# A fused RWKV-7 / short-convolution layer on one core: reordering transfers at the seam of two phases, and moving the preparation of four output weights to GpSimd

## The chip, the core and the metric

The kernel runs on one core of a Trainium2 chip. The core has five engines that each take their instructions in order: TensorE (PE in the profile, with its weight loads listed as PEld), VectorE (DVE), ScalarE (ACT), GpSimd (POOL) and SyncE (SP), which here issues nearly all transfers between the chip's memory (DRAM) and the on-chip memory (SBUF). A transfer queue is in order as well: if its next transfer has to wait, all behind it wait too. The metric is the device time of one execution, in microseconds (us), as a median over runs.

## What is computed

One layer on 128 context tokens and 2048 latent tokens of width 1024. The normalised, modulated input h goes through one input projection. Half of its channels (8 heads of 64) go through RWKV-7 mixing in both directions, the other half through a short gated convolution; both halves are gated, joined, and go through the output projection `w_out`. Cut to what matters here:

```python
def step(S, inp):                       # RWKV-7, per head, S is 64 x 64
    r_t, w_t, k_t, v_t, kk_t, a_t = inp
    s_kk = einsum('bdhij,bdhj->bdhi', S, kk_t)
    S = S * w_t[..., None, :] - s_kk[..., :, None] * (kk_t * a_t)[..., None, :] \
        + v_t[..., :, None] * k_t[..., None, :]
    return S, einsum('bdhij,bdhj->bdhi', S, r_t)
...
ya = ya * silu(g_a)                     # after a group norm and a bonus term
yb = b_gate * short_conv(c_gate * u_conv) * silu(g_b)
u = concatenate([ya, yb], -1) @ w_out
y = rmsnorm(x + gate * u)
```

The latent scans start from cached states `state_wkv`. The outputs are y of both kinds of tokens and the final states of the context.

## The kernel before

The scan is not run token by token. Tokens are cut into chunks of 64. Within a chunk the delta rule needs the inverse of a triangular 64 x 64 matrix per chunk, head and direction; between chunks only the state S is passed on. Matrix products in full precision are made of three products of a high and a low part (`hi`, `lo`), the high part being a copy into the type fp32r and the low part the difference.

**Phase 1** (`phase1`) makes the projections. The tokens stand in six blocks, taken as three pairs; for each pair the dense products of all column blocks are made (L166 to L168, tiles `mm...`), and their results are turned into the operands of the scan (`scr_ops`, `scr_at`, `scr_lo`, `scr_vt` in DRAM) or into the convolution (`convB` makes the products `mmc` and `mmu` and the taps, L523 to L541; `gateB` makes `mmgb`, `mmb` and the gates, L570 to L585). In the last pair the convolution of column groups 1, 2 and 3 stands at the very end: twelve steps, each one call of `convB` or `gateB` for one block. After each of the twelve, one step of the generator `early` of phase 2 is taken. This stretch, about 890 to 1005 us, is the seam.

**Phase 2** (`phase2`) goes through 17 stages, each of 16 chunks (two directions). Stage s needs, in order: its operands (`partL`), the inverses of 32 x 32 triangles (`partI` on GpSimd, which calls `load_I`, `solve_steps` and stores to `scr_zt`), the products F and G and their evacuation (`partW`, L1041 and L1048), the 64 x 64 inverse from the 32 x 32 ones (`partU`), X and E (`partB`), and the chain of states (`partS`, L1147). `main` has one round per stage; the letters of `ROUND` give the order in which the products of stage s and s+1 are mixed, and `mm` ties these products into one order by hand (`O.line`). The copy with a mask (L1072) stands once in every round, which makes it a mark of the rounds.

In the seam, `early` does what can be done ahead: it sets up the tiles (L785), centres the cached states (`center_states`: load L977, reduce L979, subtraction L981, store L982), lets GpSimd invert for stages 2 and 5, lets VectorE invert for stages 3 and 4 (`by_vector`, whose working space is the part of the tiles `fg` that stage 1 will use later for its operands), and does stage 0's `partW` and `partU` and some of `partB`. GpSimd's diagonal tile and the centring's mean share one buffer (tag `dgp`).

Stage 1's operands are loaded by `load_half` (L998), into the part of `fg` in which VectorE has inverted; so they wait for those inverses and for their stores (L955).

**Phase 3** (`phase3`) is the output projection in 17 tiles of 128 tokens. `ahead` prepares the weights of the convolution half during phase 2's last rounds (`load_k`: high part L1360, low part L1361, for k = 4 to 7), splits the mixed values of the first two tiles (`load_m`: L1372, L1373) and makes their products (`psa`, from L1380 on); these products are not in the hand-made order. `tail` does the rest; there the other four weights are already split by GpSimd for the low part (L1361) and ScalarE for the high part.

What sets the order: the program gives priorities by the order in which instructions are written, and a planner orders each engine's queue by simulating the program with its own costs. An instruction whose inputs are ready in that simulation can be put before others that were written earlier. `behind(r, ins)` adds an edge for the planner alone: r is not ordered before ins, though no wait is made for it on the chip. `K.dense` is the last dense product written so far. Waits on the chip follow from the data and from the reuse of buffers.

Of the kernel before, what the change touches and what calls it, by code (L numbers as in the profile page):

```python
# [6 lines left out]
F32 = mybir.dt.float32  # L7
F32R = mybir.dt.float32r
BF16 = mybir.dt.bfloat16
AF = mybir.ActivationFunctionType  # L10
ALU = mybir.AluOpType
# [743 lines left out]
def phase2(K):  # L755
    nc, tc, A, S = K.nc, K.tc, K.A, K.S
    V, G, P, T = nc.vector, nc.gpsimd, nc.scalar, nc.tensor
    D = nc.sync.dma_start
    B = Ctx()
    O = Ctx()  # L760
# [101 lines left out]
    def half(g, n):  # L862

        h = n if g.d == 0 else 1 - n
        return slice(h * 4, h * 4 + 4)
# [66 lines left out]
    def solve_steps(eng, s, ab, zt, tmp, dg, after):  # L932

        zf = zt[:].rearrange("p a b -> p (a b)")
        behind(eng.memset(zt[:], 0.0), after)
        for h in range(2):
            eng.memset(zf[h * 64:(h + 1) * 64, h:512:34], 1.0)

        eng.tensor_copy(dg[:], ab[:].rearrange("p j i -> p (j i)")[:, 1:1024:66])
        eng.tensor_scalar(zf[0:64, 1:512:34], dg[0:64], -1.0, None, ALU.mult)  # L940
        tv = tmp[:].rearrange("p (j m) -> p j m", m=16)
        eng.tensor_tensor(tv, ab[:, :, 0:32:2], dg[:].unsqueeze(1).broadcast_to((128, 32, 16)), ALU.mult)
        eng.tensor_tensor(ab[:, :, 1:32:2], ab[:, :, 1:32:2], tv, ALU.subtract)
        for m in range(15):
            j, kn, n = 2 * m, m + 1, 30 - 2 * m
            tv = tmp[:, :kn * 2 * n].rearrange("p (q r i) -> p q r i", r=2, i=n)
            eng.tensor_tensor(tv, ab[:, j:j + 2, j + 2:32].unsqueeze(1).broadcast_to((128, kn, 2, n)),  # L947
                              zt[:, :kn, j:j + 2].unsqueeze(3).broadcast_to((128, kn, 2, n)), ALU.mult)
            for r in range(2):
                last = eng.tensor_tensor(zt[:, :kn, j + 2:32], zt[:, :kn, j + 2:32], tv[:, :, r], ALU.subtract).ins  # L950
            if m % 4 == 0:
                yield
        if eng is G:
            O.solved = last
        (G.dma_start if eng is G else D)(S["zt"][s].rearrange("h u s b q i -> (h u s b) (q i)"), zf)  # L955

    def by_vector(s, d):

# [15 lines left out]
    def center_states():  # L974

        x = O.rI.tile([64, 16, 64], F32, tag="ab", name="st0", bufs=1)
        D(x[:], A["st0"].rearrange("k d h v -> k (d h) v"))  # L977
        mn = O.rI.tile([64, 16], F32, tag="dgp", name="st0mean", bufs=1)
        V.tensor_reduce(mn[:], x[:], mybir.AxisListType.X, ALU.add)  # L979
        V.tensor_scalar(mn[:], mn[:], -1.0 / 64, None, ALU.mult)  # L980
        V.tensor_tensor(x[:], x[:], mn[:].unsqueeze(2).broadcast_to((64, 16, 64)), ALU.add)  # L981
        D(S["sti"].rearrange("k d h v -> k (d h) v"), x[:])  # L982
# [8 lines left out]
    def load_half(g, us, D):  # L991

        p, c0 = g.units[us.start]
        src = S[f"ops{g.d}"][1:3]
        for h in range(2):
            dst = B.fg[g.d][H[h], :, g.op, h, us].rearrange("c k u t -> c k (u t)")
            if g.blk is not None:
                D(dst, src[:, p * 128 + h * 64:p * 128 + h * 64 + 64, c0 * 64:(c0 + 4) * 64].rearrange("k c t -> c k t"))  # L998
            else:
                for k in range(2):  # L1000
                    D(dst[:, k].rearrange("c (g t) -> c g t", t=128), src[k, :, 0:128].rearrange("(g h c) t -> h c g t", h=2, c=64)[h][:, p:p + 2])
# [9 lines left out]
    def partW(s, st):  # L1011

        D = nc.sync.dma_start if s else P.dma_start
        for g in st.g:
            g.E, g.F = [], []
            g.op = 1 + s % 2
            g.io = slice(0, g.op + 1, g.op)
            g.gs, g.fs = B.fg[g.d][:, 0], B.fg[g.d][:, 1]
        for n in range(2):
            for g in st.g:  # L1020
                load_half(g, half(g, n), D)
            if n == 0:
                if s:
                    states(s, st)
                st.zc = tl([128, 16, 32], "zc", 1, O.r0)
                for h in range(2):
                    D(st.zc[h:128:2], S["zt"][s][h].rearrange("u s b q i -> (s b q) u i"))

            def product(k, x, nm):
                ps = [ps_tile([128, 4, 128], f"ps{nm}{s}_{gi}_{n}") for gi in range(2)]  # L1030
                for i in range(4):
                    for gi, g in enumerate(st.g):
                        u = half(g, n).start + i
                        for h in range(2):
                            mm(ps[gi][place(g.d, h), i, :].rearrange("p (b t) -> p b t", b=2), g.ops[H[h], k, u, :], B.fg[g.d][H[h], x, g.io, h, u])
                return ps

            ps = product(0, 1, "F")
            for gi, g in enumerate(st.g):
                g.F.append(tl([128, 4, 128], "F", 4, O.r0))  # L1040
                V.tensor_tensor(g.F[n][:], ps[gi][:], B.mF[:, g.d].unsqueeze(1).broadcast_to((128, 4, 128)), ALU.mult)  # L1041
            yield
            ps = product(1, 0, "G")
            for gi, g in enumerate(st.g):
                us = half(g, n)
                for h in range(2):
                    r = place(g.d, h)
                    V.tensor_tensor(g.gs[H[1 - h], g.op, h, us], ps[gi][r, :, 64:128], B.mG[r, g.d].unsqueeze(1).broadcast_to((64, 4, 64)), ALU.mult)  # L1048
                    copy(g.gs[H[1 - h], 0, h, us], ps[gi][r, :, 0:64])
            yield  # L1050
# [174 lines left out]
    sts = {}  # L1225
    K.mixed = {}

    def early():
        setup_first()
        center_states()  # L1230
        partI(2)
        B.back = O.solved
        vec = (x for k in range(2) for x in by_vector(3 + k, k))
        next(vec)
        yield
        sts[0] = partL(0, K.dense)
        next(vec)
        yield
        W, uu, bb = partW(0, sts[0]), partU(0, sts[0]), partB(0, sts[0])
        for gen in (W, W, uu, uu, uu):  # L1240
            next(gen, None)
            next(vec, None)
            next(vec, None)
            yield
        partI(5, B.back)
        for gen in (bb, W, W):
            next(gen, None)
            next(vec, None)
            yield
        for _ in vec:  # L1250
            pass
        B.bb = bb

    def main():
# [85 lines left out]
def phase3(K):  # L1340
    nc, tc, A, S = K.nc, K.tc, K.A, K.S
    V, G, P, T = nc.vector, nc.gpsimd, nc.scalar, nc.tensor
    D = nc.sync.dma_start
    O = Ctx()
# [6 lines left out]
    def load_raw(k):  # L1351

        raw = O.r.tile([128, 1024], F32, tag="raw", name=f"woraw{k}", bufs=2)
        D(raw[:], A["wout"][k * 128:(k + 1) * 128, :])
        return raw

    def load_k(k, hi, lo, eng, raw=None):

        raw = raw or load_raw(k)
        P.copy(hi[:], raw[:])  # L1360
        eng.tensor_tensor(lo[:], raw[:], hi[:].bitcast(F32), ALU.subtract)  # L1361
        wk[k] = (hi, lo)

    def load_m(pool, i, ks, b):

        t0 = i * 128
        a = "c" if ks is CONV else "a"
        mx = O.r.tile([128, 4, 128], F32, tag="raw", name=f"mx{a}{i}", bufs=2)
        D(mx[:], S["mixT"].rearrange("(k p) t -> p k t", p=128)[:, ks[0]:ks[0] + 4, t0:t0 + 128])
        mh = pool.tile([128, 4, 128], F32R, tag=f"mh{a}", name=f"mh{a}{i}", bufs=b)  # L1370
        ml = pool.tile([128, 4, 128], F32R, tag=f"ml{a}", name=f"ml{a}{i}", bufs=b)
        P.copy(mh[:], mx[:])  # L1372
        V.tensor_tensor(ml[:], mx[:], mh[:].bitcast(F32), ALU.subtract)  # L1373
        return mh, ml

    def products(ps, ms, cs, ks, start, stop):
# [15 lines left out]
    def ahead():  # L1392
        yield
        for n, k in enumerate(CONV):
            load_k(k, *[K.spare(f"wo{a}{k}", F32R, f"o{k - 3}{m}") if n < 2 else O.r.tile([128, 1024], F32R, name=f"wo{a}{k}") for m, a in enumerate("hl")], V, O.raw[n])
            if n < 2:
                O.raw.append(load_raw(CONV[n + 2]))
            yield
        for i in AHEAD:
            ms = load_m(O.r, i, CONV, 1)  # L1400
            if i not in z0:
                z0[i] = K.spare(f"z0_{i}", F32, "ab2" if z0 else "ab")
            for h in range(2):
                ps = O.pr.tile([128, 512], F32, tag="u", name=f"psa{i}_{h}")
                products(ps, ms, HALF[h], CONV, True, True)
                P.copy(z0[i][:, HALF[h]], ps[:])
                yield
# [103 lines left out]
```

## Time and profile before

| | us |
|---|---|
| median of three runs | 1651.52 |
| lowest and highest run | 1651.35, 1659.19 |
| the profiled execution, whole | 1657.8 |
| its span from the first to the last instruction | 1656.0 |
| mean granted clock of TensorE | 0.969 |

| engine | busy us | share of the span | instructions |
|---|---|---|---|
| TensorE | 1538.7 | 93% | 17160 |
| VectorE | 1108.4 | 67% | 2226 |
| ScalarE | 766.8 | 46% | 1623 |
| GpSimd | 569.0 | 34% | 1028 |

How to read the profile's views. A timeline has a row per instruction or run of like instructions: start in us, us, engine, line, operation, output<-input, count, and in brackets how long the engine was idle before it and who ended the wait. Queue names end in q (SPq is the transfer queue of SyncE). The chain of waits that ended last has start, us, and what. A list of waits has who waited for whom, us in total, times, longest. A row by line has the shapes, then the busy time and the mean ns of one, then the idle time before. A row by stretch has the stretch, its length, busy us of the five engines with their counts, the granted clock of TensorE (1.00 is full speed), the share of the transfer engines, and GB/s. Who ended a wait is inferred: of several releasers it names the one that came last.

### The profile page before, as it was taken

To read this page: it belongs to the slowest core of one execution; us is meant where nothing else is said; L and a number is where in the kernel's file an instruction comes from. 1 tells how busy PE (TensorE), PEld (TensorE's weight loads), DVE (VectorE), ACT (ScalarE), POOL (GpSimd) and SP (SyncE) were. 2 spreads that over 40 slices of the span, in tenths; PEclk is the share of its full clock that TensorE was granted. 3 is DMA by queue.
4 is the path that set the end of the run, shared out by engine and by line. 5 is a ranking of instruction groups with operands and counts; after the bars stand their busy time and mean duration, and the time that the engine had idled before them with its cause. 6 is when DMAs were issued, how large, how long until landed. Compare 5 with 4: busy or idle time off the path is not lost.

```text
span 1656.0 us, 42386 instructions
## 1 busy us (share of the span) xinstructions
PE 1538.7 (93%) x17160; PEld 1412.4 (85%) x17160; DVE 1108.4 (67%) x2226; ACT 766.8 (46%) x1623; POOL 569.0 (34%) x1028
## 2 busy tenths in 40 slices
PE   5899999999999999999999899988988888789998
PEld 2899998999999999999988898878887777668886
DVE  5876977784738775658787883576775765574333
ACT  4544565553425353435554013667675665432222
POOL 0011211110102121112765564888888700022221
PEclk8899999999999999999999999999999989889999
DMA  9677767664746465655858768676767643264342
GB/s 377 205 263 249 244 234 276 218 225 178 241 140 208 166 207 183 200 202 186 271 165 270 237 201 239 179 192 180 204 175 195 169 131 102 66 198 160 127 149 93
DMA packets 237988, 327.23 MB, mean 198 GB/s; under 512 B 91288, under 2 KB 191896, under 8 KB 223712
## 3 DMA queue, kind: packets, MB, share of 16 engines
q1 hardware_dynamic: 231840, 318.55, 60.8%
q0 software_dynamic: 1200, 3.93, 0.6%
q8 instruction: 135, 2.21, 0.6%
q10 hardware_dynamic: 4752, 2.04, 0.5%
q14 instruction: 61, 0.50, 0.1%
HBM read 207.92 MB, written 116.54 MB: 196 GB/s over the span
## 4 chain that ended last, share of the span: by engine, by line
PE 47%; DVE 10%; ACT 7%; DMA 4%; issue 3%; POOL 3%; SPq 0%; DVEq 0%; ACTq 0%; POOLq 0%
PE psu L1380 4%; PE psu L1381 4%; PE psu L1382 4%; PE psE L840 3%; PE psS L840 2%; ACT fg L829 2%; PE psX L840 2%; PE psW L840 1%; PE mmg L166 1%; PE mmg L168 1%; PE mmg L167 1%; PE mmc L166 1%; PE mmc L167 1%; PE mmu L167 1%; PE mmu L166 1%
## 5 line engine op out<-in xcount | busy, mean ns | idle before, releaser
L950 POOL TENSOR_TENSOR zt<-zt,ztmp 128x30 f32<-128x30 f32 (+7 forms) x390 | 153.3, 393 | 30.6
L840 PE MATMUL psE<-fg 128*64 128x128 f32 x2176 | 135.8, 278 | 17.4 <-ACT fg L831 15.2
L840 PEld LDWEIGHTS psE<-fg 128*64 128x64 f32 x2176 | 120.8, 139 | 24.1 <-ACT fg L831 17.8
L840 PE MATMUL psS<-sv,E 128*64 128x64 f32 x2176 | 99.5, 235 | 19.3 <-DVE sv L1147 18.4
L840 PEld LDWEIGHTS psS<-sv,E 128*64 128x64 f32 x2176 | 82.5, 144 | 35.5 <-DVE sv L1147 24.4
L329 POOL TENSOR_TENSOR shk<-rawl 128x384 f32<-128x384 f32 (+1 forms) x24 | 24.8, 1033 | 242.9 <-ACT rawl L325 223.8
L829 ACT ACTIVATE fg<-psX 64x512 f32<-64x512 f32 x136 | 80.4, 591 | 44.9 <-PE psX L840 42.8
L1147 DVE TENSOR_TENSOR sv<-psS,pc 64x128 f32<-64x128 f32 x254 | 63.9, 277 | 43.6 <-PE psS L840 41.4
L947 POOL TENSOR_TENSOR ztmp<-ab,zt 128x60 f32<-128x60 f32 (+4 forms) x165 | 85.1, 516 | 12.9
L1447 POOL TENSOR_TENSOR z<-z,x 128x512 f32<-128x512 f32 x32 | 41.7, 1304 | 138.3 <-DVE z L1443 114.8
L329 POOL TENSOR_TENSOR shv<-rawl 128x384 f32<-128x384 f32 (+1 forms) x24 | 20.8, 866 | 164.5 <-ACT rawl L325 164.4
L1041 DVE TENSOR_TENSOR F<-psF,consts 128x512 f32<-128x512 f32 x68 | 44.0, 681 | 46.5 <-PE psF L840 46.5
L831 ACT COPY fg<-psG 64x256 f32<-64x256 f32 x136 | 49.8, 366 | 52.4 <-DVE fg L1048 46.3
L1048 DVE TENSOR_TENSOR fg<-psG,consts 64x256 f32<-64x256 f32 x136 | 57.3, 421 | 24.0 <-ACT fg L831 11.7
L166 PE MATMUL mmc<-h,w 128*128 128x384 f32 (+1 forms) x192 | 64.8, 337 | 5.9 <-ACT q1r L327 4.1
L446 POOL COPY pcs<-pp 128x6 f32<-128x6 f32 (+1 forms) x48 | 21.0, 437 | 139.2 <-ACT pp L435 138.9
L166 PE MATMUL mmg<-h,w 128*128 128x384 f32 (+1 forms) x192 | 64.3, 335 | 3.8 <-ACT q1v L327 3.8
L831 ACT COPY E<-psE 128x256 f32<-128x256 f32 x136 | 48.4, 373 | 37.8 <-DVE E L1109 27.9
L1109 DVE TENSOR_TENSOR E<-psE,consts 128x256 f32<-128x256 f32 x136 | 53.0, 418 | 19.0 <-PE psE L840 17.6
L166 PE MATMUL mmb<-h,w 128*128 128x384 f32 (+1 forms) x192 | 62.9, 328 | 1.5 <-ACT ta L439 1.5
L166 PE MATMUL mmgb<-h,w 128*128 128x384 f32 (+1 forms) x192 | 64.0, 333 | 0.3 <-ACT q1r L327 0.3
L168 PE MATMUL mmg<-h,w 128*128 128x384 f32 (+1 forms) x192 | 64.0, 334 | 0.0
(323 smaller groups left out, 5173.3 us busy)
## 6 DMA issues: line engine op xcount, KB each, us to landing
w<-scr_wsp SPq DMA_DIRECT2D x68, 1024.0 KB, 5.7
scr_wsp<-w SPq DMA_DIRECT2D x34, 1024.0 KB, 4.9
scr_ops<-pair SPq DMA_DIRECT2D x80, 384.0 KB, 4.0
wr<-in_win SPq DMA_DIRECT2D x34, 512.0 KB, 5.9
o<-scr_ops SPq DMA_DIRECT2D x32, 512.0 KB, 6.6
fg<-scr_ops SPq DMA_DIRECT2D x120, 128.0 KB, 3.5
x<-in_x SPq DMA_DIRECT2D x17, 512.0 KB, 8.5
wadas<-in_wada SPq DMA_DIRECT2D x8, 1024.0 KB, 13.5
```

The source lines that it names most:

```text
L166: T.matmul(ps[:, :n], w[:, 0, k], hh[:, 0, k, :n], start=k == 0, stop=False)
L168: K.dense = T.matmul(ps[:, :n], w[:, 1, k], hh[:, 0, k, :n], start=False, stop=k == 7).ins
L829: P.activation(dst, src, AF.Copy, scale=-1.0)
L831: P.copy(dst, src)
L840: r = T.matmul(*a, start=True, stop=True, **k)
L947: eng.tensor_tensor(tv, ab[:, j:j + 2, j + 2:32].unsqueeze(1).broadcast_to((128, kn, 2, n)), zt[:, :kn, j:j + 2].unsqueeze(3).broadcast_to ...
L950: last = eng.tensor_tensor(zt[:, :kn, j + 2:32], zt[:, :kn, j + 2:32], tv[:, :, r], ALU.subtract).ins
L1048: V.tensor_tensor(g.gs[H[1 - h], g.op, h, us], ps[gi][r, :, 64:128], B.mG[r, g.d].unsqueeze(1).broadcast_to((64, 4, 64)), ALU.mult)
L1147: r = V.tensor_tensor(dst, sp[gi][0:64, q], B.pc[0:64, d, 2 * p:2 * p + 2, c:c + 1].broadcast_to((64, 2, 64)), ALU.mult)
L1380: T.matmul(ps[:], mh[:, n], hi[:, cs], start=start and n == 0, stop=False)
L1381: T.matmul(ps[:], mh[:, n], lo[:, cs], start=False, stop=False)
L1382: T.matmul(ps[:], ml[:, n], hi[:, cs], start=False, stop=stop and n == 3)
```

## The change

Four edits.

The centring is a generator now. Its load is issued where it was; the reduce, the subtraction and the store come one step of `early` later, after `partL(0)` and ahead of VectorE's first inverse.

VectorE's two inverses do not store at once. The store is kept, with a counter of 3; `put_back` runs once at the end of each step of `early` from the third on, and when the counter reaches 0 it issues the store, ordered behind the last dense product written so far, which it notes in `B.mid`. By the order of the steps the first store falls behind `mmu` of column group 2, second block, the second behind `mmu` of group 3, first block.

Stage 1's loads are ordered behind these same products: the first half of direction 0 behind the first, the first half of direction 1 and both second halves behind the second.

`load_k` and `load_m`, where `ahead` calls them, use GpSimd both for the copy that makes the high part (before: ScalarE) and for the difference that makes the low part (before: VectorE). In `tail` nothing changes.

```diff
@@ solve_steps
-        (G.dma_start if eng is G else D)(S["zt"][s].rearrange(...), zf)
+        store = lambda by: by(S["zt"][s].rearrange(...), zf)
+        if eng is G:
+            store(G.dma_start)
+        else:
+            B.kept.append([3, store])
@@ center_states
         mn = O.rI.tile([64, 16], F32, tag="dgp", name="st0mean", bufs=1)
+        yield
         V.tensor_reduce(mn[:], x[:], mybir.AxisListType.X, ALU.add)
@@ partW
-                load_half(g, half(g, n), D)
+                load_half(g, half(g, n), D if s != 1 else lambda *a: behind(D(*a), B.mid[1 if n else g.d]))
@@ early
+    def put_back():
+        for x in B.kept:
+            x[0] -= 1
+        while B.kept and B.kept[0][0] <= 0:
+            behind(B.kept.pop(0)[1](D), K.dense)
+            B.mid.append(K.dense)
...
-        center_states()
+        B.kept, B.mid = [], []
+        center = center_states()
+        next(center)
...
         sts[0] = partL(0, K.dense)
+        for _ in center:
+            pass
         next(vec)
...
             next(vec, None)
+            put_back()
             yield
...
         for _ in vec:
             pass
+        while B.kept:
+            put_back()
@@ load_k
+        copy = P.copy if raw is None else G.tensor_copy
-        P.copy(hi[:], raw[:])
+        copy(hi[:], raw[:])
@@ load_m
-    def load_m(pool, i, ks, b):
+    def load_m(pool, i, ks, b, copy=P.copy, eng=V):
...
-        P.copy(mh[:], mx[:])
-        V.tensor_tensor(ml[:], mx[:], mh[:].bitcast(F32), ALU.subtract)
+        copy(mh[:], mx[:])
+        eng.tensor_tensor(ml[:], mx[:], mh[:].bitcast(F32), ALU.subtract)
@@ ahead
-            load_k(k, ..., V, O.raw[n])
+            load_k(k, ..., G, O.raw[n])
...
-            ms = load_m(O.r, i, CONV, 1)
+            ms = load_m(O.r, i, CONV, 1, G.tensor_copy, G)
```

More of the change, by code (lines that the diff above doesn't have):

```diff
@@ L954, in solve_steps @@
             O.solved = last
-        (G.dma_start if eng is G else D)(S["zt"][s].rearrange("h u s b q i -> (h u s b) (q i)"), zf)
+        store = lambda by: by(S["zt"][s].rearrange("h u s b q i -> (h u s b) (q i)"), zf)
+        if eng is G:
+            store(G.dma_start)
+        else:
+            B.kept.append([3, store])
     def by_vector(s, d):
@@ L1251, in early @@
             pass
+        while B.kept:
+            put_back()
         B.bb = bb
@@ L1394, in ahead @@
         for n, k in enumerate(CONV):
-            load_k(k, *[K.spare(f"wo{a}{k}", F32R, f"o{k - 3}{m}") if n < 2 else O.r.tile([128, 1024], F32R, name=f"wo{a}{k}") for m, a in enumerate("hl")], V, O.raw[n])
+            load_k(k, *[K.spare(f"wo{a}{k}", F32R, f"o{k - 3}{m}") if n < 2 else O.r.tile([128, 1024], F32R, name=f"wo{a}{k}") for m, a in enumerate("hl")], G, O.raw[n])
             if n < 2:
```

## The prediction

> **What bounds the kernel now.** I read the page's first part first, then the waits of each engine, then the stretches where TensorE (PE) is not full, and there the chain and the timelines of single engines.
>
> ```profile
> PE 1538.7 (93%) x17160; PEld 1412.4 (85%) x17160; DVE 1108.4 (67%) x2226; ACT 766.8 (46%) x1623; POOL 569.0 (34%) x1028
> ```
>
> PE is busy for 93% of the span, 1538.7 us of 1656.0. An edit that touches no PE instruction can therefore win only where PE waits or runs at a reduced clock. There are two such places near the change: the seam, where stage 0 of the second phase is worked in among the last dense products, and the two rounds in which the output weights of the convolution half are prepared.
>
> **The seam.** The columns of the first fence (busy time by stretch) are the stretch, its length, busy us of PE, PEld, DVE, ACT and POOL, then PE's granted clock, the DMA share and GB/s.
>
> ```profile
> 935.00:940.00 5.00, 1.25 (x8) 0.94 (x6) 4.76 (x11) 0.00 (x0) 4.29 (x10) 0.85 0.98 333
> 940.00:945.00 5.00, 4.82 (x39) 4.49 (x40) 5.00 (x13) 0.00 (x0) 4.42 (x8) 0.50 0.54 210
> ```
>
> ```profile
> 930.85 1.64 PE L840 MATMUL psF<-fg,o 64*64 64x128 f32 x32 [1.33 <-DVE fg L950]
> ...
> 940.18 2.77 PE L840 MATMUL psG<-fg,o 64*64 64x128 f32 x32 [3.92 <-DVE F L1041]
> ```
>
> PE stands still for 1.33 and 3.92 us, and in the 5 us after the second gap its clock is 0.50, which makes 2.5 us of full-speed work late. The ceiling of the seam is 1.33 + 3.92 + 2.5 = 7.75 us. The larger gap ends when VectorE has emptied psF (L1041), so VectorE's queue has to be followed back:
>
> ```profile
> 909.14 6.43 DMA scr_q<-bsum
> 915.64 5.99 DMA st<-in_st
> ```
>
> ```profile
> 921.75 1.21 DVE L979 TENSOR_REDUCE st0mean<-st 64x16 f32<-64x1024 f32 x1 [4.46 <-DMA st<-in_st]
> ...
> 924.97 0.15 DVE L939 COPY dgv<-fg 128x16 f32<-128x16 f32 x1
> 925.05 0.47 DVE L523 SCALAR_TENSOR_TENSOR ob<-rawl,dv,ob 128x256 f32<-128x256 f32 x1
> ...
> 939.45 0.68 DVE L1041 TENSOR_TENSOR F<-psF,consts 128x512 f32<-128x512 f32 x1
> ```
>
> VectorE waits 4.46 us for the load of the cached states, and that load could start only when the store at 909.14 had landed, since its tile lies in that store's memory. Behind the wait stand the last steps of one convolution (L523 among them) and VectorE's first inverse (L939 on).
>
> **Centring split.** Nothing is removed. A reduce of 1.21 us and a subtraction over the same tile, which I price alike (the scaling between them is small), fall one step back in priority, and the store of the centred states with them. The load stays where it is, so the 6.43 us store still delays it. What can pass the wait is the convolution's work, not the inverse, whose own loads come later on SP's queue than the cached states:
>
> ```profile
> 916.22 3.58 SPq L925 DMA_DIRECT2D fg<-scr_at  x4
> ...
> DMA to landing us min/median/max: 5.2/5.2/5.6
> ```
>
> The fourth of these starts about 0.42 us before 916.22 + 3.58, at 919.4, and lands 5.2 to 5.6 us later, at 924.6 to 925.0. The inverse began at 924.97. So at best it begins 0.4 us earlier, and the two convolution steps that now sit among its first instructions (L523 of 0.47 us, and L525, priced by its twin) can be done before it: 0.4 + 0.9 = 1.3 us. I take 1.1 us off the 3.92 us gap. Its upper end is the ceiling, 7.75 us gained; if the centring now lands among the inverse's steps instead, its two operations come on top of the wait and 2.4 us are lost.
>
> The dip of the clock I leave in place, because shorter gaps had one too (next fence: the clock is 0.66 in ten us that begin inside a gap of 2.00 us, whose row stands below).
>
> ```profile
> 1340.00:1350.00 10.00, 9.01 (x142) 7.81 (x144) 7.55 (x15) 7.28 (x16) 0.00 (x0) 0.66 0.32 85
> ```
>
> [...]
>
> POOL waits on the centring as well (its diagonal tile shares a buffer with the mean):
>
> ```profile
> 925.16 1.50 POOL L939 COPY dgp<-o 128x16 f32<-128x16 f32 x1 [23.64 <-DVE dgv L939]
> ...
> 927.76 1.31 POOL L942 TENSOR_TENSOR ztmp<-o,dgp 128x512 f32<-128x512 f32 x1
> ```
>
> That inverse is for stage 2, and is read in the rounds of phase 2, the first of which passes 1012.88 (row below): 88 us later. POOL is busy for 57.94 us in all between 890 and 1005 (next fence), with this and one more inverse. A start some us later costs nothing.
>
> **Loads and stores behind dense products.** Two stores of VectorE's inverses (L955) and the eight loads of stage 1 (L998) get later places on SP's queue.
>
> ```profile
> SPq L998 <- DVE fg L950: 16.8, 2, 14.0
> ```
>
> ```profile
> 982.52 0.55 DVE L541 TENSOR_TENSOR pv<-ct,mmu 128x384 f32<-128x384 f32 x1 [4.12 <-PE mmu L168]
> ...
> 1010.34 0.32 PE L840 MATMUL psF<-fg,o 64*64 64x128 f32 x2
> ```
>
> SP's in-order queue stood 14.0 us in front of a load whose target VectorE was still inverting. Behind it stood weight loads of the dense products, the loads of POOL's next inverse and a store. The wait is large, but PE paid nothing for it:
>
> ```profile
> 890.00:1005.00 115.00, 109.55 (x987) 106.46 (x988) 82.67 (x206) 19.02 (x45) 57.94 (x119) 0.97 0.75 232
> ```
>
> Of the 5.45 us that PE is idle here, 5.25 are the two gaps above, which have other causes. So the wait is worth 0. The new place must not be too late either. Six loads go behind the product whose result VectorE takes at 982.52. Let the store before them (0.5 us to issue, 5.3 to land), six issues of 0.6 us and a landing of 5.3 us follow one another: 982.5 + 0.5 + 5.3 + 3.6 + 5.3 = 997, and PE's first use is at 1010.34. The issue and landing times are the medians of these loads (next fence). There are 13 us to spare, so 0 again; if this cover were gone, each us beyond it would stop PE one for one.
>
> ```profile
> L998 SPq DMA_DIRECT2D fg<-scr_ops x16: 573/591/1237, 956.7 to 1025.6; - x16
> ...
> DMA to landing us min/median/max: 2.6/5.3/11.2
> ```
>
> **Conv weights by GpSimd.** Four casts of 128x1024 and two of 128x512 leave ScalarE; four and two subtractions leave VectorE. The rounds of phase 2 are measured from one masked copy (L1072) to the next:
>
> ```profile
> 1012.88 1.32 ACT L1072 ACTIVATE zb<-zc,consts 128x512 f32<-128x512 f32 x2
> ...
> 1316.07 1.32 ACT L1072 ACTIVATE zb<-zc,consts 128x512 f32<-128x512 f32 x2
> ...
> 1344.33 1.32 ACT L1072 ACTIVATE zb<-zc,consts 128x512 f32<-128x512 f32 x2
> ...
> 1375.70 1.32 ACT L1072 ACTIVATE zb<-zc,consts 128x512 f32<-128x512 f32 x2
> ```
>
> Twelve rounds take 303.2 us, 25.3 each. The next two take 28.3 and 31.4 us. In the second of them 2.0 us are PE's own first output products, so the excess is 3.0 + 4.1 = 7.1 us. The chain shows what it consists of:
>
> ```profile
> 1333.20 0.95 ACT woh L1360
> ...
> 1334.18 1.22 DVE wol L1361
> ...
> 1335.43 3.49 DMA woraw<-in_wout
> ...
> 1338.94 1.05 ACT woh L1360
> ...
> 1340.02 1.23 DVE wol L1361
> ```
>
> ```profile
> 1340.31 1.58 PE L840 MATMUL psF<-fg,o 64*64 64x128 f32 x32 [2.00 <-ACT E L831]
> ...
> 1370.65 1.09 PE L840 MATMUL psE<-fg 128*64 128x128 f32 x16 [2.00 <-ACT fg L831]
> ...
> 1373.72 0.79 PE L1380 MATMUL psa<-woh,mhc 128*128 128x512 f32 x1
> ```
>
> Cast, subtraction, reload of the raw buffer, cast, subtraction: 7.94 us in which ScalarE and VectorE, both in order, stood in front of evacuations that PE needed. PE waited 2.00 us at 1340.31 and again at 1370.65. With the work on POOL, I count the first round's 3.0 us as gained in full and of the second's 4.1 us some 60%, 2.4, since its clock dips have other gaps too: 5.4 us. The ends are 0 and 7.1, plus 3 more if PE's output products, ready sooner, fill gaps. POOL's price:
>
> ```profile
> 1316.00:1344.00 28.00, 22.71 (x570) 19.60 (x572) 18.23 (x44) 18.90 (x39) 1.20 (x4) 0.95 0.53 142
> ```
>
> ```profile
> L1361 POOL TENSOR_TENSOR wol<-woraw,woh 128x1024 fp32r<-128x1024 f32 x4 | 9.8, 2452 | 45.5 <-ACT woh L1360 32.8 <-ACT E L831 12.6
> L935 POOL MEMSET zt<- 128x512 f32 x10 | 5.3, 529 | 0.0
> ```
>
> A subtraction costs POOL 2.45 us where VectorE takes 1.22. No row shows POOL casting a wide tile; twice the memset of half the width (1.06) and the subtraction itself (2.45) bound it, and I take 1.3, nearer the one-input row. Four weights are then 4 x 3.75 = 15.0 us (14.0 to 19.6), two mixes at half width 3.8, so about 19 and at most 25 us. From 1333 to the first product at 1373.72 there are 40 us, and POOL is nearly empty (1.20 of 28 us in the stretch shown). This cover hides it; if it were gone, PE's output products would come later, us for us.
>
> Sum: 0 + 1.1 + 5.4 = 6.5 us. The profiled execution took 1657.8 us, 1.8 beyond its span, and would become 1651.3. It lies 6.3 us above the median of the runs, 1651.52, from which I count: 1651.5 - 6.5 = 1645.0.
>
> **The rivals.** First, collisions of POOL and VectorE eat the gain. In the seam this happens already:
>
> ```profile
> 927.69 1.46 DVE L947 TENSOR_TENSOR fg<-fg 128x60 f32<-128x60 f32 x1
> ...
> 956.47 0.21 DVE L947 TENSOR_TENSOR fg<-fg 128x60 f32<-128x60 f32 x1
> ```
>
> The same instruction takes 0.21 us alone and 1.46 beside POOL's L942. The moved work keeps POOL busy for 19 of the 57 us from 1316 to 1373, and each round has two wide VectorE operations on two SBUF operands (L1202, L1217). Of some four such, one or two would meet POOL and wait up to 2.45 us, with the state products' scaling queued behind them: 2 to 5 us back, so 1647 to 1650. Against it: most of VectorE's work there reads PSUM. [...] Chance 0.27, together with the case that rounds stay as long for other reasons.
>
> Second, both places heal fully: 7.75 + 7.1 + 1 = 16 us, 1636. For it: VectorE's order is replanned, and F may leave earlier; against it: the inverse's own load lands at 924.6 in any case. Chance 0.13.
>
> Third, slower: the planner puts the output products on PE's queue before POOL has delivered. PE is in order, so the hand-ordered products behind them wait too. The point is POOL's last mix: if the planner takes POOL to be as quick as ScalarE and VectorE were, 4 x (1.05 + 1.22) and two mixes of half that, 11.4 us, against a true 19 to 25, PE stops for 8 to 14 us, and a dip of the clock as in the seam adds 2.5. Less the 5.4 this is 5 to 11 us slower, 1657 to 1662; it is slower than now from a stop of 3 us on. For it: POOL stands nearly empty, so the planner may start early. Against it: 15 us to spare today. Chance 0.10.
>
> **How the numbers follow.** My forecast, 1645.0 with 1641 to 1649 as its own range, has 0.50. A measurement of this kernel can tell about 0.5% from no change, 8.3 us, so the bound is 1643.2. The forecast's lower part (about 0.25) and the second case give faster 0.38; the rest of the forecast and the first rival same 0.51; the third, and a misplaced centring, slower 0.11. The range reaches to the full healing and, above, past no change: 1636 to 1656.
>
> **What would show it.** After: no wait of some 14 us of SP before L998; the gap before psG between 2 and 3.5 us; two rounds before the output products near 25 and 28 us; POOL casts of about 1.3 us ending before PE's first psa. I am wrong if the gap before psG goes altogether, if PE waits on POOL, or if VectorE's two-operand rows stretch beside POOL's.

## The result, and the profile after

| | median us | runs | ratio to before, 95% interval |
|---|---|---|---|
| before | 1655.89 | 20 | |
| after | 1649.28 | 20 | 0.9962 (0.9951 to 0.9973) |
| after, once more (experiment 9) | 1648.05 | 12 | 0.9952 (0.9930 to 0.9974), before 1655.38 |

The change makes the kernel faster by 0.38% by the ratio, 6.3 us (4.5 to 8.1; the two medians differ by 6.6). That is less than the 0.5% that the prediction set as its bound; 6.5 us were forecast. The three runs of before from which the forecast counts had a median 4.4 us below that of the twenty here; hence 1649.3 and not 1645.0. The profiled execution of after took 1655.9 us (span 1654.1) and is the slowest of its twenty runs, so below a single profile tells the mechanism, and the ratio of many runs the time.

The first part of the page of after. GpSimd has gained 19.3 us of busy time on 569.0, the 19 of the forecast:

```profile
PE 1534.0 (93%) x17160; PEld 1407.2 (85%) x17160; DVE 1103.7 (67%) x2220; ACT 763.4 (46%) x1617; POOL 588.3 (36%) x1040
```

**The seam.** After, timeline of TensorE, then the stretches (columns as before):

```profile
934.64 1.81 PE L840 MATMUL psF<-fg,o 64*64 64x128 f32 x32 [3.04 <-DVE fg L950]
...
942.05 1.89 PE L840 MATMUL psG<-fg,o 64*64 64x128 f32 x32 [0.29 <-DVE F L1046]
```

```profile
930.00:935.00 5.00, 1.96 (x18) 1.72 (x16) 4.76 (x10) 0.38 (x1) 4.41 (x8) 1.00 0.57 193
935.00:940.00 5.00, 4.87 (x46) 4.54 (x44) 4.76 (x14) 0.00 (x0) 4.26 (x10) 0.66 0.65 210
```

The gap before psG is almost gone (0.29 for 3.92 us), that before psF has grown (3.04 for 1.33), and a dip of the clock follows the larger gap again. The dip now ends ahead of psG (the clock is 1.00 from 940 to 945), where in before most of it lay behind psG's start. SP's 14.0 us in front of stage 1's loads are gone too; the wait that stands there now (list of waits of SP, after) is in front of the first store of an inverse:

```profile
SPq L955 <- DVE fg L950: 6.1, 1, 6.1
```

**The conv weights.** After, timeline of ScalarE, the masked copies (now L1077):

```profile
1316.24 1.32 ACT L1077 ACTIVATE zb<-zc,consts 128x512 f32<-128x512 f32 x2
...
1339.52 1.32 ACT L1077 ACTIVATE zb<-zc,consts 128x512 f32<-128x512 f32 x2
...
1362.61 1.32 ACT L1077 ACTIVATE zb<-zc,consts 128x512 f32<-128x512 f32 x2
...
1414.03 1.32 ACT L1077 ACTIVATE zb<-zc,consts 128x512 f32<-128x512 f32 x2
```

Rounds 13 and 14 take 23.3 and 23.1 us (28.3 and 31.4 before), but round 15 takes 51.4 (40.4 before). At the start of round 15 TensorE stands still (after, timeline of TensorE, and the stretch around it):

```profile
1364.90 0.80 PE L1402 MATMUL psa<-woh,mhc 128*128 128x512 f32 x1 [4.42 <-POOL mhc L1394]
...
1367.68 0.80 PE L1404 MATMUL psa<-woh,mlc 128*128 128x512 f32 x1 [0.71 <-POOL mlc L1395]
```

```profile
1360.00:1370.00 10.00, 4.87 (x32) 2.87 (x27) 0.00 (x0) 3.69 (x7) 5.72 (x8) 0.66 0.57 117
```

The first output product waits for GpSimd's split of the mixed values; behind it on TensorE's queue wait the hand-ordered products, so VectorE is idle for ten us, and the granted clock is 0.66 on the mean of the stretch. How GpSimd came to be late is in its timeline and in that of SP's queue (both after):

```profile
1332.56 1.03 POOL L1382 CAST woh<-woraw 128x1024 fp32r<-128x1024 f32 x1 [12.20 <-PE psG L840]
1333.68 2.37 POOL L1383 TENSOR_TENSOR wol<-woraw,woh 128x1024 fp32r<-128x1024 f32 x1
1344.75 1.04 POOL L1382 CAST woh<-woraw 128x1024 fp32r<-128x1024 f32 x1 [8.70 <-DMA woraw<-in_wout]
1345.86 2.35 POOL L1383 TENSOR_TENSOR wol<-woraw,woh 128x1024 fp32r<-128x1024 f32 x1
1352.25 1.04 POOL L1382 CAST woh<-woraw 128x1024 fp32r<-128x1024 f32 x1 [4.04 <-DMA woraw<-in_wout]
1353.36 2.71 POOL L1383 TENSOR_TENSOR wol<-woraw,woh 128x1024 fp32r<-128x1024 f32 x1
...
1364.23 0.61 POOL L1394 CAST mhc<-mxc 128x512 fp32r<-128x512 f32 x1 [7.60 <-DMA mxc<-scr_mixT]
```

```profile
1335.08 5.80 SPq L1006 DMA_DIRECT2D fg<-scr_ops  x8
1340.97 0.54 SPq L1375 DMA_DIRECT2D woraw<-in_wout  x1
...
1356.40 0.55 SPq L1391 DMA_DIRECT2D mxc<-scr_mixT  x1
```

The weights and the mix share two buffers, so each load waits for the subtraction before it. The raw buffer is free at 1333.68 + 2.37 = 1336.05, but its reload stands on SP's queue behind eight loads of operands and is issued at 1340.97. From the first cast to the mix's cast done GpSimd's chain takes 32.3 us; ScalarE and VectorE needed 18.8 (1333.11 to 1351.95; before, timeline of ScalarE):

```profile
1333.11 1.04 ACT L1360 CAST woh<-woraw 128x1024 fp32r<-128x1024 f32 x1
...
1351.33 0.62 ACT L1372 CAST mhc<-mxc 128x512 fp32r<-128x512 f32 x1 [1.02 <-DMA mxc<-scr_mixT]
```

Of the 32.3 GpSimd works for 11.2, adding its rows up.

### The profile page after: what moved, and what is told of

It reads as the page before. It is cut to its first block, busy times and chain, and to the rows that moved or that the text cites. A ratio compares the mean times of both kernels' runs of the same rounds, so it can differ in the third digit from the quotient of the medians.

```text
span 1654.1 us, 42387 instructions
## 1 busy us (share of the span) xinstructions
PE 1534.0 (93%) x17160; PEld 1407.2 (85%) x17160; DVE 1103.7 (67%) x2220; ACT 763.4 (46%) x1617; POOL 588.3 (36%) x1040
## 4 chain that ended last, share of the span: by engine, by line
PE 47%; DVE 10%; ACT 6%; issue 4%; DMA 4%; POOL 2%; SPq 0%; DVEq 0%; ACTq 0%; POOLq 0%
PE psu L1402 4%; PE psu L1403 4%; PE psu L1404 4%; PE psE L840 3%; PE psS L840 2%; ACT fg L829 2%; PE psX L840 2%; PE psW L840 1%; PE mmc L166 1%; DVE E L1114 1%; PE mmu L168 1%; PE mmu L167 1%; PE mmu L166 1%; PE psG L840 1%; PE mmgb L166 1%
## 5 line engine op out<-in xcount | busy, mean ns | idle before, releaser
L950 POOL TENSOR_TENSOR zt<-zt,ztmp 128x30 f32<-128x30 f32 (+7 forms) x390 | 156.0, 400 | 30.6
L840 PE MATMUL psE<-fg 128*64 128x128 f32 x2176 | 137.4, 281 | 15.0 <-ACT fg L831 13.2
L840 PEld LDWEIGHTS psS<-sv,E 128*64 128x64 f32 x2176 | 80.4, 141 | 35.8 <-DVE sv L1152 23.5
L329 POOL TENSOR_TENSOR shk<-rawl 128x384 f32<-128x384 f32 (+1 forms) x24 | 23.3, 969 | 243.1 <-ACT rawl L325 223.8
L829 ACT ACTIVATE fg<-psX 64x512 f32<-64x512 f32 x136 | 80.5, 592 | 39.4 <-PE psX L840 37.4
L1469 POOL TENSOR_TENSOR z<-z,x 128x512 f32<-128x512 f32 x32 | 41.8, 1306 | 138.8 <-DVE z L1465 114.4
L947 POOL TENSOR_TENSOR ztmp<-ab,zt 128x60 f32<-128x60 f32 (+4 forms) x165 | 85.1, 516 | 12.9
L1053 DVE TENSOR_TENSOR fg<-psG,consts 64x256 f32<-64x256 f32 x136 | 57.4, 422 | 27.7 <-PE psG L840 12.4
L1114 DVE TENSOR_TENSOR E<-psE,consts 128x256 f32<-128x256 f32 x136 | 53.1, 418 | 22.7 <-PE psE L840 21.3
L166 PE MATMUL mmg<-h,w 128*128 128x384 f32 (+1 forms) x192 | 64.2, 334 | 3.8 <-ACT q1v L327 3.8
L166 PE MATMUL mmv<-h,w 128*128 128x384 f32 (+1 forms) x192 | 63.7, 332 | 0.3 <-ACT q1r L327 0.3
```

What stands on the lines that cost most here:

```text
L166: T.matmul(ps[:, :n], w[:, 0, k], hh[:, 0, k, :n], start=k == 0, stop=False)
L829: P.activation(dst, src, AF.Copy, scale=-1.0)
L840: r = T.matmul(*a, start=True, stop=True, **k)
L1114: V.tensor_tensor(to(H[1]), of(H[1]), B.mE[:, g.d].unsqueeze(1).broadcast_to((128, 4, 64)), ALU.mult)
```

## Experiments

Twelve runs beside before and after. The table takes one profile of each: "seam" runs from VectorE's first read of mmu of column group 1 to the last dense product, "inverse" from the first step of VectorE's inverse (L939) to its evacuation of psF, the rounds from masked copy to masked copy, the last stretch from the copy of round 16 to the end. All in us. The ratio is that of all runs of a kernel to those of the kernel before on the same chip; the ratio of the two medians differs from it by up to 0.0017. Kernels 7 and 8 ran once each (1658.50 and 1657.03 us), too little for a ratio. The expectations of 1 to 3 count the rounds from nought: their rounds 12 to 14 are 13 to 15 here.

| kernel | seam | inverse | rounds 1-12 | 13 | 14 | 15 | 16 to end | ratio (95%) |
|---|---|---|---|---|---|---|---|---|
| before | 93.3 | 14.48 | 303.2 | 28.3 | 31.4 | 40.4 | 239.9 | |
| after | 91.0 | 13.20 | 303.7 | 23.3 | 23.1 | 51.4 | 240.1 | 0.9962 (0.9951-0.9973) |
| 1 seam alone | 90.8 | 13.35 | 298.9 | 28.0 | 28.0 | 41.4 | 240.0 | 1.000 (0.9978-1.0023) |
| 2 weights alone | 92.8 | 14.48 | 300.7 | 23.3 | 25.3 | 44.5 | 239.5 | 0.9965 (0.9945-0.9984) |
| 3 after, own mix buffer | 91.1 | 13.35 | 303.8 | 23.3 | 23.7 | 40.7 | 235.0 | 0.9916 (0.9892-0.9941) |
| 4 after, three raw buffers | 90.6 | 13.24 | 314.0 | 23.3 | 23.1 | 42.3 | 233.1 | 0.9967 (0.9948-0.9986) |
| 5 before, own mix buffer | 90.8 | 14.53 | 313.4 | 28.2 | 26.5 | 41.8 | 234.9 | 0.9987 (0.9964-1.0011) |
| 6 weights, own mix buffer | 91.2 | 14.53 | 305.4 | 23.5 | 23.1 | 40.7 | 233.2 | 0.9909 (0.9879-0.9939) |
| 7 loads and stores alone | 93.4 | 14.52 | 301.6 | 27.8 | 32.8 | 39.4 | 239.6 | |
| 8 centring split alone | 91.0 | 13.35 | 299.8 | 28.7 | 31.3 | 40.7 | 239.7 | |
| 9 after again | 90.7 | 13.34 | 297.4 | 23.3 | 23.1 | 48.4 | 239.5 | 0.9952 (0.9930-0.9974) |
| 10 as 6, casts on ScalarE | 93.5 | 14.50 | 301.7 | 28.0 | 25.6 | 41.6 | 234.9 | 0.9974 (0.9958-0.9990) |
| 11 as 6, subtractions on VectorE | 91.8 | 14.52 | 306.5 | 24.3 | 27.7 | 36.8 | 234.6 | 0.9942 (0.9923-0.9962) |
| 12 as 6, subtractions twice | 93.0 | 14.54 | 302.5 | 23.3 | 23.7 | 45.2 | 240.5 | 1.0004 (0.9987-1.0022) |

**1 and 2: each part by itself.** Kernel 1 has the change's first three edits (centring, stores, loads) on the phase 3 of before; kernel 2 has its phase 3 on the phase 2 of before.

> The seam's three edits alone; the convolution's output weights are prepared by ScalarE and VectorE as before. Theory A (both parts share the gain): about 2.5 us faster than before, because psG stands later on TensorE's queue and no longer waits 3.92 us for VectorE; from the last dense product back to 848 us the stretch is 2.2 us shorter, rounds 12 and 13 keep 28.3 and 31.4 us. Theory B (all of it is the conv weights): no change, 0 us. Theory C (all of it is the seam): 6 us faster.

> The conv weights on GpSimd alone; the seam as before, with its 3.92 us wait of psG. Theory A: about 4 us faster; rounds 12 and 13 come down to some 23 us each, round 14 grows to about 50 us because psa waits on GpSimd's first mix. Theory B: 6 us faster. Theory C: 0 us.

Measured: 1.000 and 0.9965, medians 1654.91 and 1648.5 against 1656.57. The weights alone bring as much as the whole change. The seam's worth lies somewhere within 3.7 us on either side of nothing, too wide to find 1 or 2 us: C falls in both, A and B do not part. In kernel 2 TensorE's stop at the first output products is shorter than in after, 0.76 and 1.59 us for 4.42 and 0.71, which fits its longer round 14 (25.3 us for 23.1).

**3 and 4: is it the shared buffer?** Kernel 3 gives the mixed values a buffer of their own, kernel 4 a third buffer shared by all:

```diff
-mx = O.r.tile([128, 4, 128], F32, tag="raw", name=f"mx{a}{i}", bufs=2)
+mx = O.r.tile([128, 4, 128], F32, tag="mx", name=f"mx{a}{i}", bufs=2)
```
```diff
-raw = O.r.tile([128, 1024], F32, tag="raw", name=f"woraw{k}", bufs=2)
+raw = O.r.tile([128, 1024], F32, tag="raw", name=f"woraw{k}", bufs=3)
...
-O.raw = [load_raw(k) for k in CONV[:2]]
+O.raw = [load_raw(k) for k in CONV[:3]]
```

> The changed kernel with one more edit: the mixed values have buffers of their own (tag mx, 2 buffers) and no longer wait for a raw-weight buffer to come free. If the 4.42 us wait of psa on GpSimd's mix comes from the shared buffer and the late load, it goes, with the dip of the clock behind it: 4 to 7 us faster than the changed kernel, some 11 us faster than before, round 14 about 44 us. Rival: GpSimd's own work is what is late (or the planner only moves psa still earlier and it waits as long for the fourth weight): no more than the changed kernel's 6 us.

> The changed kernel with three instead of two raw-weight buffers, three weights loaded ahead, and the mixed values sharing the three. If buffer turnover (load issued late on SyncE, 4 to 8 us to land) is what makes GpSimd late, GpSimd's four weights run with one wait at most and psa finds its operands: 4 to 7 us faster than the changed kernel. Rival (GpSimd's own work is late, or the round is bound by other waits): as the changed kernel, 6 us faster than before.

Measured: 0.9916 and 0.9967. In both the stop before the first output product is gone. In kernel 3 (timeline of GpSimd) the planner splits the first mix some 330 us ahead of its first product, in round 1, where GpSimd has time:

```profile
1029.21 0.61 POOL L1394 CAST mhc<-mxc 128x512 fp32r<-128x512 f32 x1 [3.87 <-DVE sv L1152]
```

Round 15 then takes 40.7 us, and the end gains about 5 more, since the tail's first mixes no longer queue for the raw buffers: TensorE's wait for mha of 4.97 us is 0.36. In kernel 4 two weights are prepared in rounds 1 and 2 as well, and rounds 1 to 3 take 84.6 us together, for 77.0 in after and 76.5 in kernel 3: what the end gains, the beginning pays.

**5 and 6: does the buffer help without GpSimd, and without the seam?** The first diff above, applied to before and to kernel 2.

> The kernel before, with one edit: the mixed values of a tile (mx) get a buffer of their own instead of sharing the two raw buffers of the weights. VectorE and ScalarE prepare the weights as before. Theory A: the shared buffer costs only where GpSimd prepares, since the wait of PE for the mix (4.42 us in the changed kernel, with the dip of the clock behind it) does not stand in the kernel before, whose mix was cast 22 us ahead of its first product; then the time is that of before, ratio 0.998 to 1.002, and round 16 is the only place that shrinks. Theory B: the own buffer is worth some 8 us on any engine, because it is the tail's first mixes and raw weights (PE waits 4.1 us for mha there) that stop sharing; then 1648 to 1650 against 1656.6, ratio 0.995, with round 16 at 43 us instead of 50.

> The weights on GpSimd and the mix's own buffer, without the seam's edits. Theory A, the seam is worth what the traces show there, 2.2 us: 2.2 us above the kernel with all three, so a ratio of 0.993 against before. Theory B, the seam is worth nothing: 0.9916 as with all three. Theory C, the gain of the own buffer was the planner's luck in the other kernel and has nothing to do with the wait for the mix: no better than the weights on GpSimd alone, 0.9965. A and B are closer than one measurement may tell; the trace says which by the stretch from the first use of mmu of group 1 to the last dense product (93 us without the seam's edits, 91 with them).

Measured: 0.9987 and 0.9909. Kernel 6 does what A and B expected; the two cannot be told apart by time. Kernel 5 is no faster, but not for the reason that A gave: its rounds 13 to 15 and its end are 8.5 us shorter, and round 1 takes 40.7 us instead of 27.7. There the planner has put the mix's cast on ScalarE (timelines of ScalarE and of TensorE, kernel 5):

```profile
1026.39 0.62 ACT L1372 CAST mhc<-mxc 128x512 fp32r<-128x512 f32 x1 [13.76 <-DMA fg<-scr_ops]
```

```profile
1028.32 2.20 PE L840 MATMUL psS<-sv,E 128*64 128x64 f32 x32 [13.51 <-DVE sv L1147]
```

The cast needs the first of these two loads (kernel 5, timeline of SP's queue):

```profile
1019.73 0.93 SPq L1369 DMA_DIRECT2D mxc<-scr_mixT  x2
```

ScalarE, in order, stands 13.76 us before it (the wait is put down to another load, the one that landed last by the profile), the evacuations behind it wait, and TensorE stops for 13.51 us. With the same early cast on GpSimd, round 1 takes 26.9 and 26.2 us in kernels 3 and 6: nobody in that round waits for GpSimd. The engine and the buffer brought more together than apart; that the buffer alone would bring as little if the cast stood elsewhere is not shown.

**7 and 8: the seam's parts.** Kernel 7 orders loads and stores and leaves the centring whole, kernel 8 splits the centring alone.

> The seam's loads and stores behind dense products, without the centring split; weights as before. A look at the stretch from mmu of group 1 to the last dense product: 93.0 us without any seam edit, 90.8 with all. Theory A, the order of loads and stores makes the difference (through the place that the planner then finds for psG): about 91. Theory B, the centring split does: about 93. SP's 14 us in front of stage 1's loads must be gone in both.

> The centring split alone; loads, stores and weights as before. The same stretch: by theory A (loads and stores make the difference) about 93 us, and the gap before psG near 3.9; by theory B (centring) about 91. VectorE's sequence from its wait for the cached states to its first inverse should be the same as before, as it was in the changed kernel.

Measured: 93.4 and 91.0, as B has it. Yet 93 is no fixed value: eight profiles with the unsplit centring lie between 90.8 and 93.5 (mean 92.5), six with the split between 90.6 and 91.1 (mean 90.9). The column "inverse" is sharper: 14.48 to 14.54 us in all eight, 13.20 to 13.35 in all six. The orders of TensorE's, VectorE's and ScalarE's instructions in the seam are the same in all of these kernels. Of the engines' orders only GpSimd's differs: the first step of its inverse stands earlier (kernel 8, timeline of GpSimd; then of VectorE):

```profile
911.01 0.21 POOL L939 COPY dgp<-o 128x16 f32<-128x16 f32 x1 [5.98 <-DMA o<-scr_at]
```

```profile
926.99 1.48 DVE L982 TENSOR_TENSOR st<-st,st0mean 64x1024 f32<-64x1024 f32 x1
...
928.39 0.42 DVE L939 COPY dgv<-fg 128x16 f32<-128x16 f32 x1
...
931.87 0.37 DVE L947 TENSOR_TENSOR fg<-fg 128x60 f32<-128x60 f32 x1
...
941.74 0.69 DVE L1042 TENSOR_TENSOR F<-psF,consts 128x512 f32<-128x512 f32 x1
```

GpSimd's diagonal tile shares its buffer with the centring's mean. Unsplit, GpSimd gets the buffer only after VectorE's subtraction, in before at 925.16, and both engines begin an inverse 0.2 us apart (all eight profiles); split, GpSimd takes the buffer first, in kernel 8 at 911.01, and is 17.4 to 18.0 us ahead when VectorE starts (all six). VectorE's first product (L947, 128x60) takes 1.43 to 1.47 us in the eight and 0.37 to 0.51 in the six. This step and the next (L950, 128x30) are 1.8 us slower unsplit; of the others some are slower and some quicker, and 1.2 us are left in all.

**9: the changed kernel once more.**

> The changed kernel once more, as it is, for a second profile. Theory A, the stop of PE before the first output product is built into the order of the queues: again PE waits for GpSimd's mix (4.4 us in the first profile) and round 15 takes 44 to 52 us, against 40 in the kernel before. Theory B, it was an accident of that one execution: no such wait, round 15 at 41. The seam, by what the kernels with unchanged seam code showed (90.8 to 93.3 us for one and the same code): anywhere in 90.5 to 93.5. Ratio to before 0.996.

A holds (timeline of TensorE, kernel 9): the same wait, round 15 at 48.4.

```profile
1360.36 0.79 PE L1402 MATMUL psa<-woh,mhc 128*128 128x512 f32 x1 [4.34 <-POOL mhc L1394]
```

**10 and 11: which engine's relief is it?** Kernel 6 with one of the two operations on the four weights put back:

```diff
-copy = P.copy if raw is None else G.tensor_copy
+copy = P.copy
```
```diff
-load_k(k, ..., G, O.raw[n])
+load_k(k, ..., V, O.raw[n])
```

> The weights on GpSimd with the mix's own buffer and without the seam's edits, but the four wide casts of the weights back on ScalarE (1.05 us each); the subtractions stay on GpSimd. Theory A, both engines' places count, each by the time it stands in front of an evacuation that PE needs: round 13 between 23.4 and 28, near 25.5, the whole 2 us slower than with both on GpSimd. Theory B, only VectorE's 1.23 us count: round 13 stays at 23.4. Theory C, only ScalarE's casts count, since each waits there for its raw buffer: round 13 at 28.

> The counterpart: casts on GpSimd, the four subtractions back on VectorE (1.23 us each, and each must now wait for GpSimd's cast). Theory A: round 13 near 25.5. Theory B, VectorE's place counts: 28. Theory C, ScalarE's place counts: 23.4. With A, the losses of this kernel and of the one with the casts on ScalarE add up to some 5 us in round 13.

Measured: 0.9974 and 0.9942; round 13 at 28.0 and 24.3. In round 13 it is ScalarE's cast in the main, as C has it: it waits for the raw buffer to be reloaded, with TensorE's evacuation behind it (kernel 10, timelines of ScalarE and of TensorE):

```profile
1341.31 1.04 ACT L1361 CAST woh<-woraw 128x1024 fp32r<-128x1024 f32 x1 [3.59 <-DMA woraw<-in_wout]
```

```profile
1342.68 0.98 PE L840 MATMUL psF<-fg,o 64*64 64x128 f32 x26 [3.81 <-ACT E L831]
```

The cost there is not the cast's own 1.04 us but its wait of 3.59 us at the head of a queue that TensorE needs. The subtraction on VectorE costs 1 us in round 13 and more in round 14 (27.7 for 23.1); round 15 gets some of it back, 36.8.

**12: is GpSimd's work hidden?** Kernel 6 with each subtraction made twice:

```diff
-eng.tensor_tensor(lo[:], raw[:], hi[:].bitcast(F32), ALU.subtract)
+for _ in range(1 if copy is P.copy else 2):
+    eng.tensor_tensor(lo[:], raw[:], hi[:].bitcast(F32), ALU.subtract)
```

> The weights on GpSimd with the mix's own buffer and without the seam's edits, each of the four subtractions made twice: 4 x 2.37 = 9.5 us more work for GpSimd. Theory A, GpSimd's work is hidden: it stands still for 9 us before the second weight and is nearly empty, so the extra costs at most the last steps before the first output product, under 2.5 us; rounds 13 and 14 stay at 23.3. Theory B, GpSimd's subtractions block VectorE's operations on two SBUF operands: another 2 to 5 us, in rounds 13 and 14, and VectorE's rows for such operations stretch. Theory C, the chain of raw buffer, cast and subtraction decides when the output products start, and PE stops for the whole 9.5 us.

The expectation has the size of the edit wrong: the condition never holds (in Python two readings of `P.copy` are not the same object), so the tail's four weights are subtracted twice as well, 19 us of added work, not 9.5. Measured: 1.0004, about 16 us behind kernel 6 (0.95% by the two ratios). Rounds 13 and 14 stay (23.3, 23.7), without B's 2 to 5 us: B falls. Round 15 loses 4.5 us, about half of the first four's 9.5, and the stretch behind it 7.3. So A falls as well, and C is half right: TensorE's queue waits for GpSimd's last weight (kernel 12, timeline of TensorE).

```profile
1367.41 0.79 PE L1383 MATMUL psa<-wol,mhc 128*128 128x512 f32 x1 [3.00 <-POOL wol L1363]
```

## Why the prediction came out as it did

**The sum, 6.5 us, fits the 6.3 measured, but that it fits so closely is luck. Of its two terms the weights' is right in size because two errors cancel; the seam's is too small for the times to confirm, and its mechanism was another.** Two of the signs that the prediction named for being wrong were seen: TensorE waits on GpSimd, and the gap before psG went almost altogether.

*Loads and stores, 0.* Right as far as one profile tells: kernel 7 has 93.4 us, among the 90.8 to 93.5 of the kernels without the split, though SP's 14.0 us in front of stage 1's loads are gone.

*Centring split, 1.1 us.* VectorE's inverse takes 1.2 us less to reach F, but it begins 0.5 us later: the centring ahead of it now runs beside GpSimd, and its subtraction takes 1.47 us for 1.21. From the seam's start F comes 0.7 us sooner on the mean (27.9 for 28.6). The seam is 1.6 us shorter on the mean, and part of that is the clock. From psG to the last dense product the four kernels whose clock dips behind psG's start (before, 7, 10, 12: the products mmc of 128x384 take 0.52 us there, and 0.33 to 0.35 outside a dip) take 63.6 to 64.4 us, and the other ten, split or not, 61.7 to 62.2. Of the kernels with one dip, ahead of psG, the three unsplit (2, 6, 11) take 92.0 us on the mean and the six split 90.9. That is 1.1 us, but from three profiles only, and the time of kernel 1 cannot confirm so little. The step "what can pass the wait is the convolution's work" failed: not one instruction of VectorE changed its place. The prediction had the true cause in hand, the buffer that GpSimd's diagonal shares with the mean, and asked only what a later start costs. The split made an earlier start possible, and with it VectorE's first L947 and L950 were 1.8 us shorter. The forecast of 2 to 3.5 us before psG failed too, because 3.92 us was no property of the kernel: eight profiles of the unsplit centring show 0 to 3.94 us there and 1.33 to 5.14 before psF. It goes with the dip: unsplit, it is 0 to 1.98 where the clock dips ahead of this gap (2, 6, 11, 12), and 1.96 to 3.94 in the four others. That TensorE, in a dip, then reaches psG later and finds less left to wait for fits this, and so the gap's end in after need not be the split's doing. The two gaps together are 4.75 us on the mean unsplit, 2.75 split.

*The dip stays.* In after it did, at 0.66. But one gap, one dip does not hold: kernel 8 fell to 0.50 behind a gap of 2.68 us, while kernel 5 shows no dip around gaps of 3.00 and 1.96 us (stretches, kernel 5):

```profile
925.00:930.00 5.00, 3.67 (x31) 3.47 (x29) 4.79 (x9) 0.38 (x1) 4.59 (x7) 1.00 0.83 289
930.00:935.00 5.00, 3.33 (x47) 3.19 (x48) 4.79 (x13) 0.00 (x0) 4.21 (x11) 1.00 0.50 155
935.00:940.00 5.00, 3.04 (x31) 2.55 (x33) 4.83 (x12) 0.00 (x0) 4.29 (x10) 1.00 1.02 346
```

So the length of the gap alone does not decide whether a dip follows; what does is not shown.

*Conv weights, 5.4 us.* Kernel 2 gains 0.35%, 5.8 us (2.6 to 9.1), and rounds 13 to 15 together are 4.4 us shorter on the mean: 95.2 us in the three profiles of this phase 3 (after, 2, 9) for 99.6 in the four of the old one (before, 1, 7, 8). So the size holds, but by two errors of the working that cancel. First, the excess of rounds 13 and 14 was put at 7.1 us over a mean of 25.3. A better base is the round just before: round 12 takes 23.2 in before and 23.1 to 23.9 in all fourteen profiles, and with the weights on GpSimd rounds 13 and 14 take 23.1 to 25.3. The gain there was 5.0 + 8.3 - 2.0 (the output products that moved into round 15) = 11.3 us in after. Second, "this cover hides it" failed. It set GpSimd's own 19 us against 40, and left out what stands between the operations: the reloads and SP's queue. And the cover shrinks as the rounds it lies in get faster. Before, the mix was split 21.8 us ahead of its first product (1351.95 to 1373.72). The chain is 13.4 us longer, the product is due 12.7 us earlier after the first cast (40.6 us before, 32.3 less the wait of 4.42 after): 21.8 - 13.4 - 12.7 = -4.3, and TensorE waits 4.42.

*The rivals.* The third, TensorE stopping at the first output products, came true beside the forecast at 4.4 + 0.7 us plus the dip, with reloads rather than GpSimd's speed as its main part; round 15 lost 11.0 us (2.0 of them moved work) and 8.0 in the second profile. The kernel came out faster only because rounds 13 and 14 gained more than had been reckoned. The first rival, collisions in the rounds, did not act on VectorE. After, timelines of VectorE and GpSimd at the one place where two-operand work meets:

```profile
1353.16 0.67 DVE L1207 TENSOR_TENSOR y<-y,yss 128x512 f32<-128x512 f32 x1
```

The subtraction of 2.71 us shown above began 0.20 us later; VectorE kept its 0.67 us, and GpSimd took 0.35 longer than in the rows of 2.35 and 2.37. In the prediction's pair in the seam (VectorE's L947 from 927.69, GpSimd's L942 from 927.76) it was VectorE that took longer, 1.46 us for 0.21. VectorE's work that reads PSUM kept its time: in after the two L1114 at 1334.34 took 0.76 us beside GpSimd's subtraction, and the two at 1319.52, with no GpSimd operation beside them, 0.76 as well. Of the two-operand rows of before, L1202 took 0.69 us at the median and 1.11 at most (at 1106.50, with two of GpSimd's inverse steps beside it), L1217 0.69 and 1.06. The second rival, both places healing, is kernel 3 in part: 0.84%, 13.9 us, but it takes the buffer as well. GpSimd's cast took 1.03 us, priced at 1.3.

*Still open:* whether the seam's gain is in the time at all (kernels 3 and 6, with and without it, are at 0.9916 and 0.9909); whether the split moves the clock's dip ahead of psG, which it is in all six split profiles and in four of eight unsplit; and why rounds 1 to 12 take between 297 and 304 us in profiles in which nothing was edited there, as much as the whole effect of the change.

## What to carry to other kernels

Work moved to an idle engine is hidden only if the whole chain is, its loads, the buffer they wait for and the queue they are issued on, and the slack must be counted in the faster kernel, not in the old one. Move the buffer with the engine: the engine alone brought 0.35%, the buffer alone about nothing (8.5 us gained late in the kernel, 13.0 lost in round 1), both together 0.8 to 0.9% (kernels 3 and 6, the fastest here). Before a gap of a few microseconds is explained from one profile, look for a stretch that repeats (here the 14.5 us of an inverse), since the gap itself may differ by four between executions of the same instructions in the same order, and see where the clock dips.

## What the runs showed of the hardware

VectorE and GpSimd, running the same kind of steps on SBUF at the same time, delayed each other by an amount that depended on their phase: the same chain of VectorE took 14.5 us when GpSimd began its own 0.2 us after, and 13.2 to 13.4 us when GpSimd had begun 17 to 18 us before. And the delay fell on either side: VectorE's L947 grew from 0.21 to 1.46 us in before, while in round 14 VectorE kept its time and GpSimd's 2.36 us became 2.71.
